# Steps of the conditioning products, moved from the heads of the latent-attention layer to the chunks of both attention output projections

## The chip, the cores and the metric

The kernel runs on one core of one Trainium2 chip. The metric is the device time of one execution in microseconds (us). The core has five engines with queues of their own: PE (TensorE) multiplies matrices, DVE (VectorE), ACT (ScalarE) and POOL (GpSimd) work elementwise on up to 128 rows, and SP (SyncE) here only issues transfers. PSUM holds the results of PE's products, SBUF everything else that is on the chip. L551 means line 551 of the kernel.

## The reference

A residual stream x of 512 tokens and 1024 features goes through three blocks. The first has causal attention with a forget gate ("fox"), the second has latent attention ("MLA"), and behind either stands a mixture of 16 experts with two of them for each token (MoE). A third block has a recurrence and a large table of experts. In each block six vectors that depend on the conditioning c scale, shift and gate what is done:

```python
    c_act = jax.nn.silu(c)
    for i in range(DEPTH):
        mod = c_act @ w_ada[i] + b_ada[i]
        sh1, sc1, g1, sh2, sc2, g2 = [m[:, None, :] for m in jnp.split(mod, 6, axis=-1)]
        h = rmsnorm(x, mix_norm[i]) * (1.0 + sc1) + sh1
        ...
        x = x + g1 * y
        h = rmsnorm(x, ffn_norm[i]) * (1.0 + sc2) + sh2
        x = x + g2 * hier_moe(h, moe_w_grp[i], moe_b_grp[i], moe_w_rt[i], moe_b_rt[i],
                              moe_w_gate[i], moe_w_up[i], moe_w_down[i])
```

The third block does the same with c_2, cond_w_2 and cond_b_2. Here y is the attention's output, o @ w_out. What is moved are products c_act @ w_ada and silu(c_2) @ cond_w_2: 48 columns of 128 features for each block.

## The kernel before

**Layout.** x stands in SBUF with the features on partitions, in 8 chunks of 128 features by 512 tokens. Products are taken in float32 as sums of three: each operand is split into a high part (`whi`, `o_hi`, on ACT) and what is left (`wlo`, `o_lo`, on DVE or POOL), and `mm3` multiplies high by high, low by high and high by low (L124 to L126).

**Conditioning.** `ada` (L157) is a generator that makes one column at a time: SP loads a tile `ada_w` of 128 by 1024 (512 KB), and DVE multiplies it by the silu row and sums along the row, L182; two steps later DVE adds the bias, L168. That is a step. There are three tiles `ada_w`, which lie in the pool that `self.ring` names, and loads run two steps ahead. 16 of the 144 columns are made when the kernel starts. The others, 128, are made one by one by `step(n)`, which the attention heads call (L392): 76 of them from the heads of the fox layer and 52 from those of the MLA layer. These 52 are the 4 x (2 + 2 + 2 + 7) of the tuple in the last line of `mla_heads`. The silu row of c_2, which the last 48 need, is thus made in the MLA heads; it and the row of c stand in the pool `cond`, which is closed before the MLA layer's output projection.

**Attention heads.** `heads` (L358) runs 16 heads in stages that are interleaved with their neighbours': PE makes the logits S, DVE takes the row's largest (`sm_mx`, L318), ACT exponentiates to P (L321), DVE divides (L325), PE transposes P (`tr`, L334), ACT copies (`pt`, L335), PE multiplies with the values (`pv`, L352), and ACT copies the head's result to `oT` (L353). Between the stages stands the preparation of the next four heads (a quarter).

**Output projection.** `out_proj` (L535 to L553) splits oT into `o_hi` and `o_lo`, eight tiles each, and makes 8 chunks of 24 products; DVE adds each chunk to x (L551). Behind a chunk, `then` makes ready what the MoE routes by: ACT squares x (`e_sq`, L838), DVE sums (`e_acc`, L840).

**MoE.** From x's last chunk a chain of small DVE operations runs to the lists of tokens: `n_v` and `n_r` (1 / rms), `lg` (logits), the two largest, `pos`, then PE's `pv` and DVE's `lst` (L945). Among them DVE also makes the normed rows (`n_t`, L263, and `h_row`, L961). The rows go to memory (`rows`, L964), and POOL gathers an expert's rows from there by its list (`hg`, L976). Ahead of the first gather each engine reads the count of the longest list and branches (L1104, L1105) past a part for lists that overflow. The first of the experts' weights are split ahead of that branch: seven splits `whi` on ACT, four of the `wlo` on POOL, three on DVE. POOL also numbers the tokens there (`tokens`, L1146).

**Order.** The order of each engine's instructions is set when the program is built, from what is ready first and from when a pool's memory comes free; an engine takes its queue in order.

## Time and profile before

| | us |
|---|---|
| median of 3 runs (lowest, highest) | 3077.49 (3072.53, 3083.78) |
| the profiled execution's span | 3077.5 |
| PE busy in it | 2764.6 |
| DVE busy | 2363.3 |
| ACT busy | 1314.5 |
| POOL busy | 1334.4 |

A row of the timeline gives the start, the duration, the engine, the line, the operation, what is written and what is read, and in square brackets how long the engine had been idle and what it had waited for. A row of a table by stretches gives busy times of the engines within it, the mean TensorE clock that was granted (1.00 is 2.4 GHz, 0.50 is 1.2 GHz), and the share of the DMA engines' time. The stretches of this case: the fox heads run to 368 us, their output projection to 420, the routing of the first MoE to 449. The MLA heads run from 715 to 934, their output projection to 988, the second routing to 1016.

### The profile page before, as it was taken

To read this page: it belongs to the slowest core of one execution; us is meant where nothing else is said; L and a number is where in the kernel's file an instruction comes from. 1 tells how busy PE (TensorE), PEld (TensorE's weight loads), DVE (VectorE), ACT (ScalarE), POOL (GpSimd) and SP (SyncE) were. 2 spreads that over 40 slices of the span, in tenths; PEclk is the share of its full clock that TensorE was granted. 3 is DMA by queue.
4 is the path that set the end of the run, shared out by engine and by line. 5 is a ranking of instruction groups with operands and counts; after the bars stand their busy time and mean duration, and the time that the engine had idled before them with its cause. 6 is when DMAs were issued, how large, how long until landed. Compare 5 with 4: busy or idle time off the path is not lost.

```text
span 3077.5 us, 42494 instructions
## 1 busy us (share of the span) xinstructions
PE 2764.6 (90%) x14989; PEld 2247.0 (73%) x14989; DVE 2363.3 (77%) x4756; ACT 1314.5 (43%) x2352; POOL 1334.4 (43%) x926
## 2 busy tenths in 40 slices
PE   2999978997889798899889897899999999999996
PEld 2877556686545566666766687889899999999885
DVE  7998458758975686688974799999677777777777
ACT  3344437734564573532432533334333333333332
POOL 3111027633211573006850345433566666666553
PEclk9999879998899899999988998999999999999998
DMA  6775159924535795220021223565999999999893
GB/s 220 239 242 182 65 193 314 342 96 139 185 124 188 236 331 205 90 72 19 1 78 37 88 85 122 201 227 185 322 312 321 313 318 325 326 314 315 285 328 112
DMA packets 230881, 622.81 MB, mean 202 GB/s; under 512 B 32796, under 2 KB 92492, under 8 KB 227192
## 3 DMA queue, kind: packets, MB, share of 16 engines
q1 hardware_dynamic: 130960, 429.82, 41.3%
q0 software_dynamic: 45120, 154.42, 14.7%
q10 hardware_dynamic: 54568, 35.66, 4.0%
q8 instruction: 122, 2.00, 0.3%
q14 instruction: 111, 0.91, 0.1%
HBM read 562.59 MB, written 61.01 MB: 203 GB/s over the span
## 4 chain that ended last, share of the span: by engine, by line
PE 39%; DVE 20%; DMA 4%; issue 2%; ACT 1%; POOL 1%; POOLq 0%; ACTq 0%; DVEq 0%; SPq 0%
PE y L126 5%; PE y L125 5%; PE acc L124 5%; PE acc L126 5%; PE acc L125 5%; PE y L124 5%; DVE a L1906 4%; DVE a L1902 2%; DMA wraw<-in_moe_w_dn_dram 2%; DMA wraw<-in_moe_w_gu_dram 2%; DVE s_y L1367 1%; DVE s_y L1526 1%; DVE wlo L118 1%; DVE wc L1550 1%; DVE t L1774 1%
## 5 line engine op out<-in xcount | busy, mean ns | idle before, releaser
L117 ACT ACTIVATE whi<-wraw 128x1024 fp32r<-128x1024 f32 (+1 forms) x552 | 576.5, 1049 | 458.2 <-PE acc L125 288.3
L118 DVE TENSOR_TENSOR wlo<-wraw,whi 128x1024 fp32r<-128x1024 f32 x410 | 565.5, 1390 | 265.6 <-ACT whi L117 264.4
L118 POOL TENSOR_TENSOR wlo<-wraw,whi 128x1024 fp32r<-128x1024 f32 (+1 forms) x142 | 367.1, 2592 | 478.9 <-ACT whi L117 445.2
L124 PE MATMUL acc<-h_hi,whi 128*128 128x384 f32 (+1 forms) x1328 | 478.0, 360 | 11.0 <-ACT z_out L1959 6.8
L126 PE MATMUL acc<-h_hi,wlo 128*128 128x384 f32 (+1 forms) x1328 | 472.5, 356 | 3.0 <-DVE wlo L118 3.0
L125 PE MATMUL acc<-h_lo,whi 128*128 128x384 f32 (+1 forms) x1328 | 473.1, 356 | 0.0
L126 PE MATMUL y<-whi,hid_l 128*128 128x512 f32 x768 | 302.3, 394 | 0.0
L1991 POOL DMA_INDIRECT gu<-in_peer_u_dram,e x128 | 206.5, 1613 | 219.0 <-DVE gu L2000 192.0
L125 PE MATMUL y<-wlo,hid_h 128*128 128x512 f32 x768 | 301.0, 392 | 0.0
L124 PE MATMUL y<-whi,hid_h 128*128 128x512 f32 x768 | 298.2, 388 | 0.0
L124 PEld LDWEIGHTS acc<-h_hi,whi 128*128 128x128 f32 x1328 | 255.1, 192 | 29.3 <-ACT z_out L1959 7.1
L126 PEld LDWEIGHTS acc<-h_hi,wlo 128*128 128x128 f32 x1328 | 254.4, 192 | 18.4 <-DVE wlo L118 4.0
L125 PEld LDWEIGHTS acc<-h_lo,whi 128*128 128x128 f32 x1328 | 255.1, 192 | 16.7 <-issue 1.0
L1991 POOL DMA_INDIRECT gv<-in_peer_v_dram,e x128 | 191.7, 1497 | 37.6 <-issue 27.6
L2056 ACT ACTIVATE hid_h<-hid 128x384 fp32r<-128x384 f32 x128 | 67.1, 524 | 289.2 <-PE y L125 252.7
L2032 DVE SCALAR_TENSOR_TENSOR y<-gv,pz,y 128x1024 f32<-128x1024 f32 x128 | 181.2, 1416 | 0.0
L182 DVE SCALAR_TENSOR_TENSOR ada_w<-ada_w,silu 128x1024 f32<-128x1024 f32 x138 | 174.0, 1261 | 8.7 <-DMA ada_w<-in_w_ada_dram 8.6
L125 PEld LDWEIGHTS y<-wlo,hid_h 128*128 128x128 f32 x768 | 144.2, 188 | 30.3 <-DVE wlo L118 0.3
L126 PEld LDWEIGHTS y<-whi,hid_l 128*128 128x128 f32 x768 | 144.3, 188 | 29.1
L124 PEld LDWEIGHTS y<-whi,hid_h 128*128 128x128 f32 x768 | 144.2, 188 | 28.8
L124 PE MATMUL acc<-whi,h_hi 128*128 128x256 f32 x480 | 140.6, 293 | 26.9 <-ACT whi L117 18.7
L2000 DVE SCALAR_TENSOR_TENSOR gu<-gu,hrow 128x1024 f32<-128x1024 f32 x128 | 163.2, 1275 | 0.0
(671 smaller groups left out, 6246.6 us busy)
## 6 DMA issues: line engine op xcount, KB each, us to landing
ada_w<-in_w_ada_dram SPq DMA_DIRECT2D x144, 512.0 KB, 4.2
wraw<-in_moe_w_gu_dram SPq DMA_DIRECT2D x128, 512.0 KB, 10.9
wraw<-in_peer_ut_dram SPq DMA_DIRECT2D x128, 512.0 KB, 6.3
wraw<-in_peer_v_dram SPq DMA_DIRECT2D x128, 512.0 KB, 5.9
wraw<-in_moe_w_dn_dram SPq DMA_DIRECT2D x64, 512.0 KB, 12.3
p_gd<-stage SPq DMA_DIRECT2D x24, 1024.0 KB, 3.9
gt<-p_gd ACTq DMA_DIRECT2D x16, 1536.0 KB, 22.0
wraw<-in_fox_w_in_dram SPq DMA_DIRECT2D x24, 512.0 KB, 4.7
```

The costliest lines, as they stand in the source:

```text
L117: nc.scalar.activation(hi[:, :w], r[:, :w], AF.Copy)
L118: self.low = eng.tensor_tensor(lo[:, :w], r[:, :w], hi[:, :w].bitcast(F32), op=OP.subtract).ins
L124: mm(out=out, lhsT=l[0], rhs=r[0], start=start, stop=False)
L125: mm(out=out, lhsT=l[0], rhs=r[1], start=False, stop=False)
L126: mm(out=out, lhsT=l[1], rhs=r[0], start=False, stop=stop)
L182: V.scalar_tensor_tensor(r, r, 1.0, c, op0=OP.mult, op1=OP.mult, accum_out=m)
L1902: V.tensor_tensor(a1, io[:, None, :].to_broadcast([128, 8, 128]), tr[:, 0, t0:t0 + 8, None].to_broadcast([128, 8, 128]), op=OP.is_equal)
L1906: V.tensor_scalar(a2[:, t, :], io, tr[:, 1, t0 + t:t0 + t + 1], tr[:, 2, t0 + t:t0 + t + 1], op0=OP.is_equal, op1=OP.mult)
L1991: nc.gpsimd.indirect_dma_start(out=u, out_offset=None, in_=src[:, :], in_offset=bass.IndirectOffsetOnAxis(ap=e3[:, k:k + 1], axis=0))
L2000: V.scalar_tensor_tensor(u, u, 1.0, hrow, op0=OP.mult, op1=OP.mult, accum_out=z8[b][:, k % 8:k % 8 + 1])
L2032: V.scalar_tensor_tensor(y3, vs.pop(k), z8[k // 8][:, k % 8:k % 8 + 1], y3, op0=OP.mult, op1=OP.add)
L2056: nc.scalar.activation(hh, hid, AF.Copy)
```

## The change

The MLA heads are given 4 x (0 + 0 + 1 + 4) = 20 steps in place of 52. Each output projection makes two steps behind each of its 8 chunks, 16 in all; for that it names its own pool as the one that holds `ada_w`. On the last step ahead of a pool's end the loads run only one step ahead. The pool `cond` stands on the other side of SBUF, and is closed behind the MLA layer's output projection. The rest of the diff takes away comments, so that lines move down by 1 to 7 numbers.

```diff
-            while len(rs) < min(k + bufs - 1, len(cols)):
+            while len(rs) < min(k + (bufs - 1 if self.prefetch else 1), len(cols)):
...
-    def step(self, n):
-        for _ in range(n):
+    def step(self, n, last=False):
+        for k in range(n):
+            self.prefetch = not last or k < n - 1
             next(self.aside)
...
-                self.step((k + 1) * n // 4 - k * n // 4 if k < 4 else 0)
+                self.step((k + 1) * n // 4 - k * n // 4 if k < 4 else 0, last and k == 3)
...
-    def out_proj(self, x, oT, w, g1, pool, then=None):
+    def out_proj(self, x, oT, w, g1, pool, then=None, steps=0):
+        self.ring = pool
         o = self.split(oT, pool, "o")
...
             nc.vector.scalar_tensor_tensor(x[:, c, :], ps, g1[:, c:c + 1], x[:, c, :], op0=OP.mult, op1=OP.add)
+            self.step(steps, c == 7)
+        self.ring = None
...
-        self.heads(quart, oT, pool, (2, 2, 2, 7), 2, rest)
+        self.heads(quart, oT, pool, (0, 0, 1, 4), 2, rest)
...
-                self.out_proj(x, oT, self.A["fox_w_out"], mod[:, 16:24], p, then=then())
+                self.out_proj(x, oT, self.A["fox_w_out"], mod[:, 16:24], p, then=then(), steps=2)
...
-            self.cond.close()
             with self.pool("m_out") as p:
-                self.out_proj(x, oT, self.A["mla_w_out"], mod[:, 16:24], p, then=then())
+                self.out_proj(x, oT, self.A["mla_w_out"], mod[:, 16:24], p, then=then(), steps=2)
+        self.cond.close()
...
-        cond = self.cond.enter_context(self.pool("cond", "right"))
+        cond = self.cond.enter_context(self.pool("cond"))
```

Three places show how the built program's queues moved. The first is DVE in the MLA heads, about the eighth head, where a quarter's queries are prepared (`rq`, `qk_ss`). Before:

```order
L168 TENSOR_TENSOR mod_116<-bias,ada_t 128x1
L182 SCALAR_TENSOR_TENSOR ada_w,ada_t<-ada_w,silu 128x1024
L323 RECIPROCAL sm_r<-sm_s 128x1
L168 TENSOR_TENSOR mod_116<-bias,ada_t 128x1
L182 SCALAR_TENSOR_TENSOR ada_w,ada_t<-ada_w,silu 128x1024
L740 TENSOR_TENSOR rq<-acc,mla_gq 128x384 x2
L325 TENSOR_SCALAR P<-P,sm_r 128x512
L168 TENSOR_TENSOR mod_116<-bias,ada_t 128x1
L182 SCALAR_TENSOR_TENSOR ada_w,ada_t<-ada_w,silu 128x1024
L168 TENSOR_TENSOR mod_116<-bias,ada_t 128x1
L182 SCALAR_TENSOR_TENSOR ada_w,ada_t<-ada_w,silu 128x1024
```

And now:

```order
L326 RECIPROCAL sm_r<-sm_s 128x1
L321 TENSOR_REDUCE sm_mx<-S 128x1
L326 RECIPROCAL sm_r<-sm_s 128x1
L328 TENSOR_SCALAR P<-P,sm_r 128x256
L321 TENSOR_REDUCE sm_mx<-S 128x1
L326 RECIPROCAL sm_r<-sm_s 128x1
L328 TENSOR_SCALAR P<-P,sm_r 128x384
L747 TENSOR_TENSOR rq<-acc,mla_gq 128x384 x2
L321 TENSOR_REDUCE sm_mx<-S 128x1
L326 RECIPROCAL sm_r<-sm_s 128x1
L328 TENSOR_SCALAR P<-P,sm_r 128x512
```

No step is left there: DVE's queue holds the 20 that remain ahead of the fifth head's last `sm_mx`, where 18 of the 52 stood before.

The second is PE at the end of the fox layer's heads, where the last head's `tr` and `pv` meet the first chunk of the output projection (`acc`). Before:

```order
L124 MATMUL acc<-o_hi,whi 128x512 x2
L334 MATMUL tr<-ident,P 128x128 x3
L125 MATMUL acc<-o_lo,whi 128x512
L126 MATMUL acc<-o_hi,wlo 128x512
L124 MATMUL acc<-o_hi,whi 128x512
L334 MATMUL tr<-ident,P 128x128 x4
L125 MATMUL acc<-o_lo,whi 128x512
L126 MATMUL acc<-o_hi,wlo 128x512
L124 MATMUL acc<-o_hi,whi 128x512
L125 MATMUL acc<-o_lo,whi 128x512 x2
L352 MATMUL pv<-pt,v 64x512
```

And now:

```order
L337 MATMUL tr<-ident,P 128x128 x7
L858 MATMUL tr<-wr_117,mod_114 128x20 x8
L355 MATMUL pv<-pt,v 64x512
L355 MATMUL pv<-pt,v 64x384
L355 MATMUL pv<-pt,v 64x256
L355 MATMUL pv<-pt,v 64x128
L125 MATMUL acc<-o_hi,whi 128x512 x2
L126 MATMUL acc<-o_lo,whi 128x512
```

The whole first chunk now stands behind the last head's `pv`, because `o_hi` and `o_lo` lie in memory that the heads' `pt` takes up (the pool `cond` pushed them there); ACT's and DVE's splits of oT moved with it. At the end of the MLA heads it stood so before already.

The third is POOL between the fox heads (`qk_two`) and the branch of the first MoE. Before:

```order
L118 TENSOR_TENSOR wlo<-wraw,whi 128x1024 x4
L1084 MEMSET y_zero 128x1024
L932 IOTA io_4480 128x104
L1146 IOTA tokens 128x512
L1104 TENSOR_LOAD cnt_i
```

And now:

```order
L1091 MEMSET y_zero 128x1024
L939 IOTA io_4561 128x104
L1153 IOTA tokens 128x512
L119 TENSOR_TENSOR wlo<-wraw,whi 128x1024 x4
L1111 TENSOR_LOAD cnt_i
```

The four splits moved from the output projection to behind `tokens`, into the routing. ACT's seven `whi` moved with them, two of them right behind the logits' `lt` and at least three behind the issue of the rows, and DVE's three `wlo` stand right ahead of the branch now. The reason is SP's queue, where the loads of these weights stand behind those of the 16 steps, in memory that the projection's tiles leave. At the second MoE the moves are the same.

## Rows read from the trace of the kernel before

**Rows 1.** Stretch, length; PE, PEld, DVE, ACT, POOL busy; PEclk; DMA; GB/s.

```profile
814.73:898.57 83.84, 70.66 (x315) 43.20 (x316) 73.71 (x207) 46.61 (x127) 15.37 (x10) 0.88 0.52 165
898.57:924.04 25.47, 23.44 (x114) 12.92 (x115) 10.78 (x33) 17.06 (x48) 0.00 (x0) 1.00 0.22 74
```

**Rows 2.** The same stretch, DVE's L182 alone.

```profile
814.73:898.57 83.84, 31.84 (x52) 0.88 0.52 165
```

**Rows 3.** What PE waited for from 814.73 to 898.57: us, times, longest.

```profile
PE tr L334 <- DVE P L325: 10.4, 4, 3.6
```

**Rows 4.** Timeline, PE and DVE, from the last fox head to the projection.

```profile
363.47 0.60 PE L334 MATMUL tr<-ident,P 128*128 128x128 f32 x4
...
371.56 0.75 DVE L551 SCALAR_TENSOR_TENSOR x<-acc,mod,x 128x512 f32<-128x512 f32 x1 [1.96 <-PE acc L126]
...
377.55 0.62 PE L851 MATMUL tr<-wr,mod 128*128 128x20 f32 x4
```

**Rows 5.** Timeline, PE and DVE, the same place of the MLA layer.

```profile
926.94 0.63 PE L334 MATMUL tr<-ident,P 128*128 128x128 f32 x4 [1.55 <-DVE P L325]
...
929.20 4.06 PE L352 MATMUL pv<-pt,v 128*64 128x512 f32 x8
...
941.05 0.75 DVE L551 SCALAR_TENSOR_TENSOR x<-acc,mod,x 128x512 f32<-128x512 f32 x1 [1.51 <-PE acc L126]
```

**Rows 6.** Timeline, DVE, one chunk of the fox output projection and the next's start.

```profile
398.74 0.75 DVE L551 SCALAR_TENSOR_TENSOR x<-acc,mod,x 128x512 f32<-128x512 f32 x1 [3.07 <-PE acc L126]
...
400.54 0.69 DVE L840 TENSOR_TENSOR e_acc<-e_acc,e_sq 128x512 f32<-128x512 f32 x1 [1.05 <-ACT e_sq L838]
401.49 1.23 DVE L118 TENSOR_TENSOR wlo<-wraw,whi 128x1024 fp32r<-128x1024 f32 x1 [0.26 <-ACT whi L117]
405.50 0.75 DVE L551 SCALAR_TENSOR_TENSOR x<-acc,mod,x 128x512 f32<-128x512 f32 x1 [2.79 <-PE acc L126]
```

**Rows 7.** Timeline, POOL and DVE side by side, in that projection and in the MLA heads.

```profile
402.48 11.00 POOL L118 TENSOR_TENSOR wlo<-wraw,whi 128x1024 fp32r<-128x1024 f32 x4 [66.29 <-ACT whi L117]
407.96 6.60 DVE L118 TENSOR_TENSOR wlo<-wraw,whi 128x1024 fp32r<-128x1024 f32 x2
...
729.54 0.73 POOL L596 TENSOR_TENSOR rp<-rq,sin 128x256 f32<-128x256 f32 x1
729.65 0.65 DVE L142 TENSOR_TENSOR qk_r_z<-qk_r_y 128x16 f32<-128x16 f32 x1
```

**Rows 8.** Timeline, all engines, the first MoE's routing.

```profile
419.02 0.75 DVE L551 SCALAR_TENSOR_TENSOR x<-acc,mod,x 128x512 f32<-128x512 f32 x1 [2.06 <-PE acc L126]
...
435.07 0.47 DVE L263 SCALAR_TENSOR_TENSOR n_t<-x,n_a,acc 128x256 f32<-128x256 f32 x1
...
435.62 0.66 DVE L961 COPY h_row<-S 128x512 f32<-128x512 f32 x1
...
436.36 3.03 ACTq L964 DMA_DIRECT2D rows<-h_row  x4
...
443.89 0.16 DVE L945 CAST lst<-pv 104x16 int32<-104x16 f32 x1
...
448.68 1.08 POOL L976 DMA_INDIRECT hg<-rows,lst  x1 [26.03 <-issue]
...
455.19 1.28 ACT L986 ACT_TABLE_LOAD   x1 [18.56 <-PE tr L984]
...
461.18 2.39 POOL L118 TENSOR_TENSOR wlo<-wraw,whi 128x1024 fp32r<-128x1024 f32 x1 [4.09 <-ACT whi L117]
```

**Rows 9.** Timeline, DVE and POOL, the second MoE's list and first gather.

```profile
1011.78 0.17 DVE L945 CAST lst<-pv 104x16 int32<-104x16 f32 x1
1016.09 1.11 POOL L976 DMA_INDIRECT hg<-rows,lst  x1 [25.50 <-DVEq L1105]
```

**Rows 10.** Part 6 of the page: loads of a step, KB each, us to landing.

```profile
ada_w<-in_w_ada_dram SPq DMA_DIRECT2D x144, 512.0 KB, 4.2
```

**Rows 11.** As in the first group, in the first MoE.

```profile
540.00:560.00 20.00, 19.31 (x95) 13.86 (x94) 16.37 (x19) 16.63 (x23) 14.91 (x9) 1.00 1.03 343
```

More of the change, by code (lines that the diff above doesn't have):

```diff
@@ L30, in __init__ @@
         self.ring, self.more, self.over, self.extra, self.turn, self.ahead = None, None, None, {}, {}, {}
+        self.prefetch = True
         self.holds, self.hold = [], None
```

## The prediction

> **What bounds the kernel now.** I read the busy shares first: PE is busy for 2764.6 of 3077.5 us, DVE for 2363.3, so neither is the bound everywhere, and what the change is worth must be read where it acts. Then I cut the MLA heads into stretches [rows 1]. In the later one, where no step is made, three heads take 25.47 us, 8.49 each, with PE at 23.44 of 25.47 and at full clock: PE sets the pace. From 814.73 to 898.57 seven heads take 83.84 us, and DVE is busy for 73.71 of them, PE for 70.66 at a mean granted clock of 0.88. The longest waits of PE there are for P, which DVE divides late [rows 3], since it has 26 steps in its queue (52 instructions of L182, two for each) [rows 2]. Both lose: PE waits, and what it does afterwards runs at the lower of its two clocks. Then I read the places the steps go to. In a projection's chunk, 6.76 us from one x to the next, DVE is busy for 0.75 + 0.69 + 1.23 = 2.67 us [rows 6], so there is room for two steps. Last I read what comes behind, the routing, in which a single chain decides when the first gather starts, and the MoE behind it, which has no slack to catch up: in its middle DMA is busy throughout (1.03) and PE for 19.31 of 20 us [rows 11]. So a later first gather is paid in full.
>
> **The MLA heads: -13 us (-18 to -4).** Before the fifth head ends, 20 steps stand where 18 stood, so I give the stretch to 814.73 nothing. From there to 898.57, 26 steps go: 31.84 us of L182, 1.22 each [rows 2], and an addition of about 0.17 each (the size of `lst` in [rows 8]), 4.4 us. DVE falls from 73.71 to some 37 of 84 us. Then PE is the bound. Its 70.66 us at clock 0.88 are 62.2 at full clock; with the 8% that it idles in the stretch without steps (2.03 of 25.47, [rows 1]) that is 67.6 us, 16.2 less than now. That is nearly the best case; the quarters' preparation stays, with its long way over DVE and POOL, and some of the low clock with it. The lower bound is that only the wait on P is cut, by less than half of its 10.4 us [rows 3]: -4. I take -13, nearer to the stretch without steps, because DVE will be as idle as it is there for half the heads.
>
> **The end of the fox heads: +4 (0 to +6).** Now the first chunk's products fill PE while the last head's P is made; from the last `tr` to the first x it takes 371.56 - 363.47 = 8.1 us [rows 4]. After the change all 24 products stand behind `pv`, which is the form that the MLA layer has now, and there the same takes 941.05 - 926.94 = 14.1 [rows 5], with `pv` itself at the lower clock (4.06 us). The difference is 6.0, less about 2.0 for four repeats of `tr<-wr,mod`, which leave the projection's middle: one such row of four takes 0.62 [rows 4], and there are sixteen. The MLA layer's end has that form before and after: nothing.
>
> **Steps in the projections: +3 (0 to +7).** Two steps cost DVE 2 x (1.22 + 0.17) = 2.8 us a chunk; with 2.67 that is 5.5 of 6.76. It fits on the mean, and PE hides it, as long as each `wlo` comes before PE needs it. In the new order some `wlo` stand behind two steps; I allow one stall of about the 1.4 us of a step in either projection. A step's 512 KB land in 4.2 us [rows 10], and two of them have a chunk of 6.76 us: nothing. In the fox projection ACT also makes silu of c_2, with a table load of 1.28 us more [rows 8]; ACT's own work on a chunk is a square and a split, each about as long as DVE's part of it, so that it has the room: nothing.
>
> **The two routings: +5 and +6 (-2 to +12 each).** This is what speaks most against the change. Seven splits leave the projections and stand in the routing. The profile shows what that does to DVE: while POOL ran four splits back to back, two `wlo` on DVE took 6.60 us instead of 2 x 1.23, and while POOL ran operations of 0.73 us, one of DVE's smallest took 0.65 [rows 7] instead of the 0.16 of `lst` [rows 8]: it waits until POOL's instruction is done. What has an operand in PSUM, as x, keeps its 0.75: that at 405.50 stands in the middle of POOL's four [rows 6]. The chain `n_v`, `n_r`, `lg` is of such small operations in SBUF, and POOL's first two splits of 2.39 us [rows 8] fall on it: +4.8. The third falls on the later chain, and I count it in full: +2.4. On the other side a `wlo` of 1.23 no longer stands ahead of `n_v`, and in the first routing four copies `h_row` of 0.66 and two `n_t` of 0.47 [rows 8] move behind `pos`: -1.2 and -3.6. One more table load on ACT, ahead of `ge`, costs 1.3 [rows 8]. The first list, at 443.89 now, comes 4.8 + 2.4 - 1.2 - 3.6 + 1.3 = 3.7 later. But the rows can be sent only behind the copies that moved: the last goes some 3 us behind the list, where it now goes ahead of it (436.36, [rows 8]), and a transfer of that size takes some 4.2 us to land [rows 10]; from list to gather there are 4.8 us [rows 8]. So the gather is bound by the list or by the rows, between +3.7 and 3.7 + 3 + 4.2 - 4.8 = +6.1: +5. In the second routing the copies stay ahead of the list: 4.8 + 2.4 - 1.2 = +6 on 1011.78 and on the gather at 1016.09 [rows 9]. The ends: if POOL's splits fall where DVE waits anyway, as at `pv`, the routing gets shorter by up to 2; if ACT also waits for the weights behind `lt`, +12.
>
> A rule bears on this. The Trainium skill, "SBUF — State Buffer", section "Who interferes with whom", says that DVE and GpSimd share one pair of SBUF ports, which is locked for a whole instruction, and that a DVE operation with two inputs in SBUF then waits, while a reduction or one with a single SBUF input does not. The 6.60 us in [rows 7] agree with it. By that rule the reductions and the `n_t` of the later chain would pass, the third split would cost nothing there, and the sum would be 2 x 2.4 less: 3078 in place of 3082.
>
> **Sum.** -13 + 4 + 3 + 5 + 6 = +5 us on a span of 3077.5, which is also the median of the runs (3077.49): 3082.5.
>
> **Rivals.** (1) *Faster, 3066.* POOL's splits find gaps. What speaks for it: DVE waits for PE and ACT in the routing too, the `n_t` with an operand in PSUM pass, and copies leave the first chain. Then the routings cost nothing, -16 + 4 + 1 + 0 = -11. Against it: the chain has hardly a gap ahead of `lg`, just where two splits become ready. It decides by when the first `wlo` on POOL starts: it is true if that is before `n_v` or behind `lg`. (2) *Slower, 3093.* The weights come late. They are loaded behind the last steps' tiles now, by my estimate from about 413 us, and the branch needs all seven splits; ACT's last three stand behind the rows. If ACT's two `whi` behind `lt` (some 2.5 us behind x's last chunk at 419.02, [rows 8]) wait for their load, `ge` and every `h_f` stand behind them, and the gather comes 10 to 12 us later in either routing: -13 + 4 + 3 + 11 + 11 = +16. It decides at a landing of 421.5. For it: 16 steps' loads and the last weights share the queue; against it: there are 8 us, and a load lands in 4.2 [rows 10]. (3) *The steps were not what held the heads, 3091.* PE then still waits for the preparation's way over POOL, the heads give 4, and the sum is -4 + 4 + 3 + 11 = +14. For it: the clock falls where a quarter is prepared. (4) *The change does not do what it says*, so that the same steps stay in the heads: the built order excludes that, no step stands behind the fifth head.
>
> **How the numbers follow.** 0.3%, 9.2 us, is about what a measurement of this kernel can tell from no change. My sum lies inside it with 4 us to its upper bound, so that much of its own spread is slower. I give the sum as it stands 0.46, rival 1 0.22, rival 2 0.20, rival 3 0.12. All of rival 1 is faster, rivals 2 and 3 and 0.02 of the sum's own spread are slower: faster 0.22, same 0.44, slower 0.34. The range reaches to rival 1 and rival 2 and a little beyond: 3064 to 3096.
>
> **What would show it.** After the change: seven heads from the fifth on in about 70 us, at a clock near 1.00; x at 6.8 us a chunk in both projections; from the last fox `tr` to the first x 12 to 14 us; POOL's splits between 422 and 441 us with `n_r` and `lg` stretched beside them; from x's last chunk to the first gather 34 to 36 us in the first layer instead of 448.68 - 419.02 = 29.7 [rows 8], and as much more in the second. I am wrong if the gather is not later (then POOL's splits do not meet the chain), or if the seven heads still take over 78 us (then something else than steps holds P).

## The result: slower, and where the time went

The changed kernel takes 3102.63 us (median of 4 runs, 3090.01 to 3116.11) against 3080.64 of the kernel before (4 runs, 3072.53 to 3089.66): a ratio of 1.0065, with an interval from 1.0036 to 1.0095. It is slower by about 20 us. The forecast was 3082.5, and the time lies above the range's end of 3096. Its profiled execution has a span of 3088.3 us, 10.8 more than that of before.

The page of the changed kernel opens with the busy time, share of the span and instructions of each engine:

```profile
PE 2756.0 (89%) x14989; PEld 2240.0 (73%) x14989; DVE 2365.4 (77%) x4756; ACT 1316.5 (43%) x2354; POOL 1319.6 (43%) x926
```

PE is busy for 8.6 us less than before, DVE for 2.1 and ACT for 2.0 us more, so no engine has much more work; what grew is waiting. To find it I cut both traces at the same events and compare the lengths. The table gives the core's times in us; the events are the starts of `x`, the residual of a projection's chunk, of `hg`, the first gather of an MoE, and of `oT`, the end of a head.

| stretch | before | after | difference | forecast |
|---|---|---|---|---|
| start to the last fox `oT` | 367.6 | 370.4 | +2.8 | 0 |
| to the first `x` | 3.9 | 8.4 | +4.5 | +4 |
| to the eighth `x` | 47.5 | 45.2 | -2.3 | +1.5 |
| to the first gather | 29.7 | 37.5 | +7.8 | +5 |
| first MoE, to the latent rows | 239.0 | 244.9 | +5.9 | 0 |
| MLA: to the end of the first head | 68.5 | 76.7 | +8.2 | |
| MLA: four more heads | 58.5 | 51.1 | -7.4 | 0 with the line above |
| MLA: the seven heads behind | 83.8 | 70.3 | -13.5 | -13 |
| MLA: the last four | 34.7 | 33.5 | -1.2 | 0 |
| to the first `x` | 7.8 | 8.4 | +0.6 | 0 |
| to the eighth `x` | 45.9 | 45.2 | -0.7 | +1.5 |
| to the second gather | 29.1 | 34.2 | +5.1 | +6 |
| second MoE, to the third block | 233.4 | 236.3 | +2.9 | 0 |
| the rest | 1828.0 | 1826.1 | -1.9 | 0 |

The first line varies by itself, and another profile of the kernel before has 363.8 there; but its last head belongs to the change, as is shown below. The two MoEs' lines are the ones for which the forecast has no price.

**The heads.** The windows of the changed kernel below have the columns of [rows 1]; they run to the end of the first head, over four more, and over the seven behind them. The second fence is the last of them with L183 alone, the line that was L182 in [rows 2]:

```profile
706.43:783.10 76.67, 58.66 (x320) 46.55 (x318) 65.25 (x174) 31.35 (x82) 27.53 (x20) 0.93 0.41 129
783.10:834.23 51.13, 44.77 (x214) 29.86 (x213) 44.97 (x134) 30.24 (x82) 14.61 (x10) 0.93 0.39 123
834.23:904.52 70.29, 63.81 (x314) 38.91 (x315) 39.13 (x121) 45.84 (x126) 11.26 (x10) 1.00 0.03 8
```

```profile
834.23:904.52 70.29, 0.00 (x0) 1.00 0.03 8
```

The seven heads have no step, DVE is busy for 39.13 us instead of 73.71, the granted clock is 1.00 instead of 0.88, and they take 70.29 us instead of 83.84 [rows 1]. PE's wait for the P that DVE divides, at the head of its list before [rows 3], is gone. The head of the list is now a wait for ACT, which frees S when it has made P from it, and it is short (us, times, longest):

```profile
PE S L795 <- ACT P L324: 3.6, 4, 1.2
PE tr L337 <- ACT st L790: 1.6, 5, 0.4
```

**The end of the fox heads.** PE's timeline and the first `x`, as in [rows 4]:

```profile
362.49 0.69 PE L337 MATMUL tr<-ident,P 128*128 128x128 f32 x4 [0.48 <-DVE P L328]
362.97 3.44 PE L858 MATMUL tr<-wr,mod 128*128 128x20 f32 x16
366.35 4.04 PE L355 MATMUL pv<-pt,v 128*64 128x512 f32 x8
371.72 0.73 PE L125 MATMUL acc<-o_hi,whi 128*128 128x512 f32 x2 [1.33 <-ACT o_hi L538]
378.81 0.74 DVE L556 SCALAR_TENSOR_TENSOR x<-acc,mod,x 128x512 f32<-128x512 f32 x1
```

It now has the form of the MLA layer's end [rows 5]: the router's transposes, `pv` of 4.04 us, 1.33 us in which PE waits for the split of oT, and then all 24 products. The table's 4.5 us, from the last head's `oT` on, are not all of it, since that `oT` is late itself. These are the last two heads' `oT`, first before and then in the changed kernel:

```profile
358.94 0.59 ACT L353 ACTIVATE oT<-pv 64x512 f32<-64x512 f32 x1 [4.48 <-PE pv L352]
367.62 0.59 ACT L353 ACTIVATE oT<-pv 64x512 f32<-64x512 f32 x1 [1.30 <-PE pv L352]
```

```profile
358.44 0.59 ACT L356 ACTIVATE oT<-pv 64x512 f32<-64x512 f32 x1 [1.83 <-PE pv L355]
370.42 0.59 ACT L356 ACTIVATE oT<-pv 64x512 f32<-64x512 f32 x1 [6.55 <-PE pv L355]
```

Up to the head before the last the changed kernel is 0.5 us ahead; the last head then takes 11.98 us instead of 8.68. From the last but one `oT` to the first `x` it is 20.37 instead of 12.62, so the end of the heads costs 7.8 us, 3.3 of which stand in the table's first line. All three profiles of the changed kernel have 11.98 or 11.99 for the last head, both of the kernel before 8.5 to 8.7.

**The first routing.** POOL, DVE and ACT, as in [rows 8]:

```profile
424.02 0.75 DVE L556 SCALAR_TENSOR_TENSOR x<-acc,mod,x 128x512 f32<-128x512 f32 x1 [4.55 <-PE acc L127]
426.39 1.99 ACT L118 ACTIVATE whi<-wraw 128x1024 fp32r<-128x1024 f32 x2
427.37 0.16 DVE L255 TENSOR_SCALAR n_v<-misc 128x4 f32<-128x4 f32 x1 [1.15 <-PE misc L214]
428.37 4.66 POOL L119 TENSOR_TENSOR wlo<-wraw,whi 128x1024 fp32r<-128x1024 f32 x2
428.37 0.16 DVE L145 SCALAR_TENSOR_TENSOR n_r_y<-n_r_z,n_r_y 128x4 f32<-128x4 f32 x1
428.56 2.19 DVE L143 TENSOR_TENSOR n_r_z<-n_r_y 128x4 f32<-128x4 f32 x1
430.79 2.26 DVE L144 SCALAR_TENSOR_TENSOR n_r_z<-n_r_z,n_v 128x4 f32<-128x4 f32 x1
433.28 0.16 DVE L143 TENSOR_TENSOR n_r_z<-n_r_y 128x4 f32<-128x4 f32 x1
433.94 0.24 DVE L871 TENSOR_TENSOR lg<-S,n_r_y 128x80 f32<-128x80 f32 x1
448.42 5.40 ACTq L971 DMA_DIRECT2D rows<-h_row  x4
450.54 0.16 DVE L952 CAST lst<-pv 104x16 int32<-104x16 f32 x1
454.96 3.50 DVE L119 TENSOR_TENSOR wlo<-wraw,whi 128x1024 fp32r<-128x1024 f32 x3 [1.47 <-ACT whi L118]
461.55 1.08 POOL L983 DMA_INDIRECT hg<-rows,lst  x1 [11.31 <-issue]
471.43 1.62 PE L991 MATMUL tr<-ident,hg 104*128 104x104 f32 x8 [18.73 <-DMA hg<-rows,lst]
```

Beside POOL's two splits two operations of 128x4 elements take 2.19 and 2.26 us; the first of them takes 0.16 when it comes again at 433.28. The list comes 26.52 us behind `x`, against 443.89 - 419.02 = 24.87 [rows 8], so that part is only 1.65 late. From list to gather it is 11.01 us against 4.79 [rows 8]. What POOL waits for last ahead of the gather is DVE, until 460.55: DVE's branch stands behind its three splits (454.96 to 458.46), these behind ACT's `whi`, and those behind the issue of the rows. The last rows have landed by 458.53. And then comes what I had no term for: the gathered rows reach PE's `tr` 471.43 - 461.55 = 9.9 us after the gather is issued. Before it was 5.5, as this row with 448.68 of [rows 8] says:

```profile
454.19 1.62 PE L984 MATMUL tr<-ident,hg 104*128 104x104 f32 x8 [10.43 <-DMA hg<-rows,lst]
```

What runs beside it is in the DMA share and the GB/s of the windows (last two columns): first the kernel before around its gather, then the changed kernel around both of its own.

```profile
448.00:455.00 7.00, 0.81 (x5) 0.84 (x6) 0.81 (x2) 0.00 (x0) 2.08 (x2) 0.50 0.41 123
```

```profile
455.00:472.00 17.00, 0.57 (x4) 0.61 (x5) 4.34 (x5) 1.82 (x2) 2.07 (x2) 0.50 0.79 264
1025.00:1037.00 12.00, 0.70 (x4) 0.73 (x5) 0.72 (x2) 0.00 (x0) 2.02 (x2) 0.50 0.94 298
```

The gather used to run nearly alone; now it shares the DMA engines with the loads of the MoE's next weights. In the second window of after 68.7% of the engines' span goes to the queue of the loads and 24.3% to that of the gathers. PE has no other work meanwhile: 0.70 us of 12. All thirteen profiles of this document agree on it. In 12 of their 26 routings packets of the loads run between the gather's issue and PE's `tr`, and take 70 to 77% of the engines' time there: the landing takes 9.5 to 11.2 us. In the other 14 that queue has no packet there: 5.0 to 6.3 us.

**Why the loads are there.** The section on the change says that `o_hi` and `o_lo` lie in memory of the heads' `pt`. That was wrong; the addresses in the built program say what is right. A step in a projection needs its tiles `ada_w` in the projection's own pool, three of them. Two end at byte 152544 of a partition. The third reaches to 156640, over the start of the fox heads' pool (153568) and over the first tile of the MoE's weights (from 153120). By the third tile alone the pool's first loads are placed behind the fox heads, with the split of oT behind the last head's `pv`, and in both layers the weights' loads are placed behind the last step. (In the MLA layer `o_lo` lies over the heads' pool, before and after.) So 3.5 KB of a partition, shared by one tile of the steps and one of the weights, push the whole queue of weights back. The kernel with two tiles, below, shows that it is this tile.

### The profile page after: what moved, and what is told of

Same layout as the page of the kernel before. It is cut to its first block, busy times and chain, and to the rows that moved or that the text cites. A ratio compares the mean times of both kernels' runs of the same rounds, so it can differ in the third digit from the quotient of the medians.

```text
span 3088.3 us, 42493 instructions
## 1 busy us (share of the span) xinstructions
PE 2756.0 (89%) x14989; PEld 2240.0 (73%) x14989; DVE 2365.4 (77%) x4756; ACT 1316.5 (43%) x2354; POOL 1319.6 (43%) x926
## 4 chain that ended last, share of the span: by engine, by line
PE 39%; DVE 19%; issue 2%; DMA 2%; POOL 2%; ACT 1%; POOLq 0%; ACTq 0%; DVEq 0%
PE y L127 5%; PE y L126 5%; PE acc L126 5%; PE acc L127 5%; PE y L125 5%; PE acc L125 5%; DVE a L1913 4%; DVE a L1909 2%; DVE s_y L1374 1%; DMA wraw<-in_moe_w_dn_dram 1%; DVE s_y L1533 1%; DVE wlo L119 1%; POOL wlo L119 1%; DVE wc L1557 1%; DVE t L1781 1%
## 5 line engine op out<-in xcount | busy, mean ns | idle before, releaser
L119 DVE TENSOR_TENSOR wlo<-wraw,whi 128x1024 fp32r<-128x1024 f32 x410 | 558.9, 1374 | 257.6 <-ACT whi L118 254.6
L125 PE MATMUL acc<-h_hi,whi 128*128 128x384 f32 (+1 forms) x1328 | 476.8, 359 | 10.8 <-ACT z_out L1966 6.5
L126 PEld LDWEIGHTS acc<-h_lo,whi 128*128 128x128 f32 x1328 | 254.2, 191 | 16.3 <-issue 0.8
L1998 POOL DMA_INDIRECT gv<-in_peer_v_dram,e x128 | 191.0, 1492 | 37.6 <-issue 27.3
L183 DVE SCALAR_TENSOR_TENSOR ada_w<-ada_w,silu 128x1024 f32<-128x1024 f32 x138 | 173.6, 1259 | 15.6 <-DMA ada_w<-in_w_ada_dram 12.9
L127 PEld LDWEIGHTS y<-whi,hid_l 128*128 128x128 f32 x768 | 144.3, 188 | 29.1
```

Source lines behind the costliest of these rows:

```text
L119: self.low = eng.tensor_tensor(lo[:, :w], r[:, :w], hi[:, :w].bitcast(F32), op=OP.subtract).ins
L125: mm(out=out, lhsT=l[0], rhs=r[0], start=start, stop=False)
L126: mm(out=out, lhsT=l[0], rhs=r[1], start=False, stop=False)
L127: mm(out=out, lhsT=l[1], rhs=r[0], start=False, stop=stop)
L183: V.scalar_tensor_tensor(r, r, 1.0, c, op0=OP.mult, op1=OP.mult, accum_out=m)
L1998: nc.gpsimd.indirect_dma_start(out=u, out_offset=None, in_=src[:, :], in_offset=bass.IndirectOffsetOnAxis(ap=e3[:, k:k + 1], axis=0))
```

## The experiments

My theory behind the result, A in the expectations, was that the steps themselves hide in the projections, that the heads keep their gain, and that the loss comes from the third tile: the end of the fox heads, the late splits and the late loads. The rivals there blame the steps, wherever they stand, or the splits on POOL. Each ratio below is against the kernel before on the same chip. The table has the stretches of the one above, for the profiled execution of each kernel: the MLA heads in one sum, with the first in brackets, and behind each gather its landing, from the issue to PE's `tr`.

| kernel | fox `oT` to `x` | eight `x` | gather | its landing | first MoE | MLA heads (first) | eight `x` | gather | its landing | span | ratio |
|---|---|---|---|---|---|---|---|---|---|---|---|
| before | 3.9 | 47.5 | 29.7 | 5.5 | 239.0 | 245.5 (68.5) | 45.9 | 29.1 | 5.2 | 3077.5 | |
| after | 8.4 | 45.2 | 37.5 | 9.9 | 244.9 | 231.6 (76.7) | 45.2 | 34.2 | 10.5 | 3088.3 | 1.0065 |
| mla_only | 3.9 | 47.5 | 29.9 | 5.5 | 238.6 | 244.2 (67.4) | 45.2 | 34.2 | 10.2 | 3079.4 | 1.0054 |
| fox_only | 9.0 | 45.9 | 37.7 | 9.9 | 247.9 | 243.3 (76.8) | 45.9 | 29.7 | 5.5 | 3111.3 | 1.0086 |
| two_tiles | 3.9 | 54.5 | 37.4 | 5.2 | 240.3 | 236.7 (77.4) | 50.5 | 31.7 | 5.2 | 3092.8 | 1.0042 |
| light_heads | 3.9 | 47.5 | 30.1 | 5.0 | 239.6 | 232.2 (65.1) | 45.9 | 29.8 | 6.3 | 3067.7 | 0.9976 |
| dve_splits | 8.4 | 45.2 | 31.9 | 9.6 | 243.4 | 235.9 (76.1) | 45.9 | 31.9 | 10.1 | 3091.5 | 1.0064 |
| held | 8.4 | 45.2 | 37.5 | 9.5 | 245.6 | 227.3 (60.7) | 45.2 | 34.3 | 10.0 | 3088.8 | 1.0044 |
| two_held_dve | 3.9 | 48.6 | 34.5 | 5.4 | 241.1 | 226.3 (63.1) | 46.7 | 30.9 | 5.1 | 3070.6 | 0.9977 |
| held52 | 3.9 | 47.5 | 29.9 | 5.5 | 242.2 | 243.9 (63.6) | 45.9 | 29.8 | 5.5 | 3092.9 | 1.0003 |

**The same kernel again**, beside the next three.

> The changed kernel once more, to see what lies between its profiled execution (span 3088.3 us, 10.8 over before) and the median of its runs (22 over). If the difference between its executions is noise of the MoE's or the third block's transfers, a second profile has the same times up to the second routing (last fox oT to x(7) 53.6 us, x(7) to the first gather 37.5 us, gather to the latent rows 245 us) and differs behind it. If one of the moved pieces varies, one of those three differs by several us. The ratio to before should be 1.003 to 1.008.

Measured: 3101.29 us against 3084.35, 1.0074 [1.0053, 1.0095], 6 runs. The loss stands. Its profile (span 3096.6) has the same stretches from the first `x` to the second gather within 1 us; it is 3.8 us longer in the second MoE and 3.1 in the third block. Its gathers land in 10.5 and 11.2 us.

**Only two tiles in the projections**, so that the pool reaches over neither the heads' pool nor the weights. The loads then run one step ahead instead of two.

```diff
-            while len(rs) < min(k + (bufs - 1 if self.prefetch else 1), len(cols)):
-                r = self.ring.tile([128, D], F32, tag="ada", bufs=bufs, name="ada_w")
+            n = self.tiles or bufs
+            while len(rs) < min(k + (n - 1 if self.prefetch else 1), len(cols)):
+                r = self.ring.tile([128, D], F32, tag="ada", bufs=n, name="ada_w")
...
-        self.ring = pool
+        self.ring, self.tiles = pool, 2
```

> As the change, but the projections' pool has two tiles ada_w instead of three, so that it ends 568 bytes short of where the heads' pool and the MoE's weights begin, and laps over neither. Theory A (the third tile's overlap did the harm: it pushed the first chunk, the weights' loads and the splits back): from the last fox oT to x(7) 51 to 53 us, x(7) to the first gather 29 to 31 us in both layers, gather to the latent rows 239 us, the heads keep their gain of 14: 3062 to 3068 us by the profile, ratio 0.994 to 0.998. Theory B (the steps' own 2.8 us of DVE and 1 MB of loads for each chunk did it): no better than the change, 3088 or more, ratio 1.003 or more.

Measured: 3093.77, 1.0042 [1.0017, 1.0067]. What A says of the tile came true: the end of the fox heads is back at 3.9 us (the last head at 8.5), and the gather's landing at 5.2. But the gain did not come, because the weights then arrive early again and POOL's splits meet the steps. POOL and DVE in the fox projection:

```profile
404.67 9.15 POOL L119 TENSOR_TENSOR wlo<-wraw,whi 128x1024 fp32r<-128x1024 f32 x3 [62.90 <-DMA ada_w<-in_w_ada_dram]
404.82 3.43 DVE L184 SCALAR_TENSOR_TENSOR ada_w<-ada_w,silu 128x1024 f32<-128x1024 f32 x1
408.18 3.39 DVE L184 SCALAR_TENSOR_TENSOR ada_w<-ada_w,silu 128x1024 f32<-128x1024 f32 x1
413.83 0.74 DVE L557 SCALAR_TENSOR_TENSOR x<-acc,mod,x 128x512 f32<-128x512 f32 x1
...
465.93 1.08 POOL L984 DMA_INDIRECT hg<-rows,lst  x1 [32.74 <-SPq L1113]
```

A step's product takes 3.43 us there instead of 1.22, two in a row hold `x` back, and the eight `x` take 54.5 us instead of 47.5. The first gather stays late as well, at 37.4 us, though its list is on time, 24.9 us behind `x` as before: now the loads of the weights run beside the rows that the gather reads. The last rows are issued at 454.96 and landed at 464.80, when POOL's wait for them ends, and the last three take 8.7 to 10.6 us; in the changed kernel the last took 5.0, with no load beside it. So A in that form fell: the third tile is one part of the loss, and without it the early weights cost elsewhere, POOL's splits beside the steps and the loads beside the rows. With three tiles these two are absent, since the weights come too late to meet them.

**Steps in one projection only**, with 36 left in the heads.

```diff
-        self.heads(quart, oT, pool, (0, 0, 1, 4), 2, rest)
+        self.heads(quart, oT, pool, (1, 1, 2, 5), 2, rest)
```

together with `steps=2` taken from the fox projection (mla_only) or from the MLA projection (fox_only).

> 16 steps go to the MLA layer's projection alone, and 36 stay in its heads, 4 x (1 + 1 + 2 + 5). The third tile laps over the second MoE's weights alone. Theory A: fox layer, first routing and first MoE as before; heads gain about half, 5 to 8; second routing 5 later: 3073 to 3079 us. Theory B: the loss is that of one projection's steps: about half of the change's 11 to 20, with the heads' half gain in it: 3080 to 3088.

> 16 steps go to the fox layer's projection alone, and 36 stay in the MLA heads. Theory A: x(7) 5 later, first gather 8 more, first MoE 6 more, heads gain 5 to 8, second routing as before: 3088 to 3092 us, as slow as the whole change or slower. Theory B: half of the change's loss, 3080 to 3088.

Measured: mla_only 3095.07, 1.0054 [1.0033, 1.0074]; fox_only 3111.45, 1.0086 [1.0054, 1.0118]. The profiles put each cost where its steps stand: mla_only has the late gather (34.2) and the slow landing (10.2) in the second layer alone, fox_only has 9.0, 37.7 and 9.9 in the first, and in the second 29.7 and 5.5 as before. The heads gain 1 to 2 us with 36 steps, not the 5 to 8 that A expects, and less than the 4.1 by which two profiles of the kernel before differ there. So both times are above A's (3073 to 3079, and 3088 to 3092). fox_only also shows something that belongs to the heads: its first MLA head ends late (76.8), that of mla_only does not (67.4). mla_only's profiled execution is the fastest of its six, and its ratio is worse than its profile's 2 us by an amount that no stretch of that profile explains. Of the 33.8 us that fox_only's span is longer, 9.8 stand in the third block, which no edit touches.

**Fewer steps, none of them in the projections.** Its expectation says what is left out.

```diff
-                self.out_proj(x, oT, self.A["mla_w_out"], mod[:, 16:24], p, then=then(), steps=2)
+                self.out_proj(x, oT, self.A["mla_w_out"], mod[:, 16:24], p, then=then())
```

and the same in the fox projection.

> The heads of the change, 4 x (0 + 0 + 1 + 4) steps, and none in the projections: 32 columns of the third block's conditioning are left out and stand at zero. It measures what the heads alone gain. The row of c_2 is again made among the heads, so that by the built order 6 steps stand ahead of the first head and not 8. Theory C (the change's first head came 8 us later, 76.7 instead of 68.5 from the latent rows, because silu of c_2 was ready and more steps slipped into the first quarter's preparation): latent rows to first head 67 to 69, to the last head 222 to 228 instead of 245.6, all else as before, 3055 to 3062 us. Theory D (the first head is late for another reason, such as the pools' places): again 76 to 78, 231 to the last head, 3062 to 3067.

Measured: 3073.06 against 3078.91, 0.9976 [0.9958, 0.9994]. With the projections, routings and MoEs as before, 20 steps in the heads are worth 13.3 us of their span (245.5 to 232.2), which is the term of the forecast, measured alone. Against the second profile of the kernel before, with 241.5, it is 9.3, and the medians of the runs differ by 5.9. The span, 3067.7, is above the 3055 to 3062 that I expected. The first head is at 65.1: here its silu is made in the heads again.

**The first expert's splits on DVE instead of POOL**, in both layers.

```diff
-            w = self.weight(A["moe_w_gu"][l, e, k], eng=nc.gpsimd if k == 3 or (first and k < 3) else None, key=(e, k))
+            w = self.weight(A["moe_w_gu"][l, e, k], eng=nc.gpsimd if k == 3 and not first else None, key=(e, k))
```

> As the change, with the first expert's splits on DVE instead of POOL, so that POOL runs no split in the routing. If POOL's splits hold up the chain (my prediction's step): n_v to lg takes 2.4 us instead of 6.6, and the list stands 22 to 23 us behind x(7) instead of 26.5 in the first layer; the gather 33 to 35 us behind x(7) instead of 37.5, unless the rows or the branch, ahead of which DVE now has seven splits, bind it. If the chain is held by something else, n_v to lg stays 6 to 7 us. Total 3083 to 3089 by the profile.

Measured: 3093.21, 1.0064 [1.0035, 1.0093]. DVE, POOL and PE in the first routing:

```profile
427.19 0.16 DVE L255 TENSOR_SCALAR n_v<-misc 128x4 f32<-128x4 f32 x1 [1.15 <-PE misc L214]
429.63 0.24 DVE L871 TENSOR_TENSOR lg<-S,n_r_y 128x80 f32<-128x80 f32 x1
455.78 1.08 POOL L983 DMA_INDIRECT hg<-rows,lst  x1 [27.56 <-issue]
465.38 1.62 PE L991 MATMUL tr<-ident,hg 104*128 104x104 f32 x8 [15.76 <-DMA hg<-rows,lst]
```

From `n_v` to `lg` it is 2.4 us again instead of 6.6, so POOL's splits are shown to stretch that part of the chain. The gather comes 31.9 us behind `x` instead of 37.5, but in the first layer the list is only 0.6 us earlier, since DVE now makes three splits of 1.22 us ahead of it. The other 5.0 us lie between list and gather, where the rows go out 6 us earlier and DVE reaches its branch earlier. In the second layer the list is 3.2 us earlier and the gather 2.3. So moving the splits brings the gathers forward, and only the second layer's gain is the chain's. The landing stays at 9.6 us, since the loads still run beside it. In the profiled execution the 5.6 and 2.3 us that the routings gave are used up by the last heads (+4.1, and the third profile of the changed kernel has the same 37.6 there) and the second MoE (243.1 us), and the ratio is that of the changed kernel. The span is above the 3083 to 3089 that I expected. So the gain in place is shown, a gain in time is not.

**No step ahead of the first score**: the steps of the MLA heads are held in the order behind the `sm_mx` of the head they were placed at.

```diff
-            nc.vector.tensor_reduce(mx, s[:, :n], axis=AX.X, op=OP.max, negate=True)
+            self.mark = nc.vector.tensor_reduce(mx, s[:, :n], axis=AX.X, op=OP.max, negate=True).ins
...
-                self.step((k + 1) * n // 4 - k * n // 4 if k < 4 else 0, last and k == 3)
+                with self.tc.issue_after(self.mark) if steps[0] == 0 else contextlib.nullcontext():
+                    self.step((k + 1) * n // 4 - k * n // 4 if k < 4 else 0, last and k == 3)
```

> As the change, but each step of the MLA heads is queued on DVE behind its own head's largest value: none stands ahead of the first head, one each in heads 9 to 12, four each in the last four. Theory C: latent rows to first head 60 to 68 us instead of 76.7, to the last head 220 to 228 instead of 231.6; all else as in the change; 3078 to 3084 us by the profile. Theory D: first head at 76 as in the change, and the last four heads slower by the steps: 3088 to 3092.

Measured: 3090.07, 1.0044 [1.0022, 1.0067]. The stretch to the end of the first head, L183 alone, in the changed kernel and then here:

```profile
706.43:783.10 76.67, 12.17 (x19) 0.93 0.41 129
```

```profile
710.10:770.70 60.60, 0.00 (x0) 0.97 0.27 84
```

It shrinks from 76.7 to 60.7 us. The changed kernel has 19 records of L183 there (two for each step), the kernel before 14 of L182. The fox projection makes silu of c_2 ahead of the MLA layer, so nothing holds these steps any more, and more of them are placed ahead of the first head's scores, on DVE's way to the queries. Of the 16 us the four heads behind give back 6.2, and the last four 5.2, so that the time is above the 3078 to 3084 that I expected.

**All three together**: two tiles, held steps, splits on DVE.

> Two tiles in the projections (no overlap), steps held to their heads, and the first expert's splits on DVE, so that POOL's do not meet the steps' products in the projections. If the three causes are the third tile, the steps in the preparation, and POOL's splits against DVE's steps: fox oT to x(7) 51 to 54 us (58.4 with two tiles and POOL's splits), x(7) to the gather 30 to 33, latent rows to the last head 220 to 228, last head to x(7) 54 to 56; 3058 to 3068 us, ratio 0.993 to 0.998. If it is the steps' load on DVE and DMA in any form, the projections stay at 56 or more and the total over 3075.

Measured: 3072.71 against 3078.91, 0.9977 [0.9958, 0.9995], 12 runs. The interval just excludes 1, so it is faster than the kernel before, and by way of that than the changed kernel (1.0065 and 1.0074). The first gather and its landing in it:

```profile
456.35 1.08 POOL L985 DMA_INDIRECT hg<-rows,lst  x1 [30.89 <-SPq L1114]
461.79 1.62 PE L993 MATMUL tr<-ident,hg 104*128 104x104 f32 x8 [16.17 <-DMA hg<-rows,lst]
```

The heads give 19.2 us; the routings still cost 4.8 and 1.8, and the projections 1.1 and 0.8. In the first routing POOL's last wait is for the rows: the last of them is issued at 446.42 and landed at 455.31, 8.9 us later, again with loads of weights beside it. Its time is above the 3058 to 3068 that I expected.

**All 52 steps in the heads, but held**: heads (3, 3, 3, 4), none in the projections.

> No step in the projections; all 52 stay in the MLA heads, 4 x (3 + 3 + 3 + 4), each queued on DVE behind its own head's largest value, and the pool cond on the side the change gave it. If what matters is where the steps stand and not how many there are: the projections, routings and MoEs as in the kernel before, latent rows to first head 60 to 65 instead of 68.5, and the sixteen heads 168 to 177 us (177.1 before): 3066 to 3076 us. If the heads need fewer steps: 3076 to 3086, with the heads at 178 or more.

Measured: 3085.79 against 3084.54, 1.0003 [0.9981, 1.0025]. The heads take 243.9 us, 1.6 less than before, and from the first head's end to the last's 180.3 us, above the 168 to 177 that I expected. The first head gains (63.6), the fifth to eleventh still have their steps. The first five heads together take 127.3 us (127.0 before), the seven behind them gain 7.3, and the last four lose 5.4. So moving the 52 steps within the heads moves the time among them and hardly changes the sum.

**Both kernels once more**, one run each on that chip.

> The kernel before once more, for a second profile: how far do its stretches repeat? From the second gather to the third block's first product 233 to 234 us if that stretch is steady and the 236 to 240 of the change are its own; 233 to 240 if it only varies from run to run. Latent rows to first head 68 to 69, first gather to latent rows 239 to 240.

> The changed kernel for a third profile. If both MoE stretches are longer in it by their own (the weights come late): first gather to latent rows 244 to 246, second gather to the third block 236 to 241. If they only vary: values down to 239 and 233 as in the kernel before.

Measured: 3080.06 and 3091.82. The stretches to the second gather repeat within 4.2 us in each; behind it the same kernel differs from run to run (the second MoE of the kernel before takes 233.4 and 236.2 us).

**What stays open.** Three profiles of the changed kernel have a mean span of 3091.7, two of the kernel before 3077.9: 13.8 us. The timed difference is 22 us on one chip and 17 on another. The stretches above account for the 10.8 us of the first pair, and two_held_dve, which takes the third tile, the steps ahead of the first score and POOL's splits away together, is below the kernel before in time as well. Where the rest of the timed difference lies, no profile shows: behind the second gather the stretches vary from run to run, and the third block took 1828.1 and 1832.0 us before and 1826.1, 1829.2 and 1822.3 after. I have no run that ties that rest to a cause.

## Why the prediction was wrong, step by step

**Heads, -13: right.** 245.5 to 231.6 is -13.9, the seven heads in 70.3 us at a clock of 1.00. The seven repeat (82.4 in the second profile before, 70.3 in all three after), the sixteen less well: the means of all profiles, 243.5 and 233.2, differ by some 10. The step "to the fifth head: nothing" came out at +0.8 as a sum, +8.2 and -7.4, but for a reason that it does not give, and held shows that it hides a possible gain.

**End of the fox heads, +4: too small,** and wrong in the cause that the section on the change names. From the last `tr` to the first `x` it is 378.81 - 362.49 = 16.3 us where 12 to 14 were forecast, and from the last but one `oT` on it is +7.8. The forecast took the transposes `tr<-wr,mod` off as leaving the projection's middle. They do leave it, but now stand ahead of `pv`, where they take 3.44 us; and two steps of 1.22 us stand on DVE ahead of the first `x`. two_tiles, with `o_hi` where it was and only the third tile gone, has the last head and the 3.9 us of before.

**Projections, +3: too much.** They got shorter by 3.0, since the transposes left the fox layer's and the splits left both, and the steps hid, as the chunk of 6.8 us said they would. From the last but one `oT` to the eighth `x` the fox layer is 5.5 longer, which is the forecast of both terms, 4 + 1.5, by luck: the end is dearer than forecast and the projection cheaper. The bound of a stall behind two steps is real, but only where POOL splits at the same time (two_tiles, +7.0).

**Routings, +5 and +6: +7.8 and +5.1.** In the second the pieces can be read one by one: `n_v` 0.6 earlier, `n_v` to `lg` 4.2 longer (forecast 4.8), from `lg` to the list 0.7 longer (forecast 2.4 for the third split), and 0.75 more from list to gather. Beside that third split one small operation, `e_e`, takes 1.18 us instead of 0.17, while the `n_t` beside it, with an operand in PSUM, keep 0.47. The rule that I weighed, the Trainium skill, "SBUF — State Buffer", section "Who interferes with whom", says that only an operation that needs DVE's second port waits; the trace agrees, and by it the third split's price would have been nearer. In the first routing the list was only 1.65 late, and the last rows are issued 3.3 us behind it (forecast 3) and landed 5.0 later (forecast 4.2, [rows 10]). But neither list nor rows set the gather, as the prediction says: POOL's last wait is for DVE, until 460.55, 2.0 us behind the rows' landing. The prediction has no term for the three splits that DVE makes ahead of the branch, which stand behind the rows by way of ACT's queue.

**The MoEs, 0: the step that failed.** The prediction says that a later first gather is paid in full, and its sum has no term for anything else that changes behind it. The first half holds, the second does not: the gather itself lands in 9.9 and 10.5 us instead of 5.5 and 5.2, because the loads that the third tile pushed behind the branch run beside it. The first MoE is 5.9 us longer, the second 2.9, with the landing's 4.4 and 5.3 in them. mla_only and fox_only show this in the layer that has steps and in that alone, two_tiles in none. The lengths agree over all profiles: with the slow landing the first MoE takes 243.4 to 247.9 us and the second 236.3 to 243.1, without it 238.6 to 242.2 and 232.4 to 236.2. The prediction knew that the weights are loaded late (rival 2) and looked for the cost in ACT's `whi` ahead of the list; those ran without a wait, at 426.39. The mechanism was priced in the wrong place.

**The sum.** Heads and routings came out with the sign and about the size that were forecast. The end of the fox heads and the projections did not, and their errors cancel: -13.9 + 7.8 - 3.0 + 7.8 + 5.1 = +3.8 in the profile instead of +5, close by luck. The missing term adds 8.8, the rest of the table -1.8, and the profile is 10.8 longer. None of the rivals came true by its own sign: POOL's first split, at 428.37, falls between `n_v` and `lg` (1), ACT's `whi` did not wait (2), and the heads gave 14 (3). The missing term alone would have put the forecast at 3091, inside its range, and the profiled execution is inside it too (3090.01). It is the fastest of its four, and their median is 12.6 higher: by that spread the time left the range, and what makes it stays open.

## What to carry to other kernels

Work that is moved takes its buffers along: look where they lie, since a few KB that reach over another pool can reorder a whole queue of loads and everything that hangs on it. Price what is pushed aside to the end, past the wait that you are looking at: a load that comes late costs again as the neighbour of the next transfer that the bound engine waits for. And a gain that is right in its place (14 us in the heads) has to be held against each place that the work goes to; here, of the forms that were tried, the same move pays only with two tiles, the splits off POOL and the steps behind the first score together, and then by 0.2%.

## What the runs showed of the hardware

A gather of 104 rows took 5.0 to 6.3 us from issue to PE's first use where no backlog of loads ran (14 routings; 123 GB/s around it in the kernel before), and 9.5 to 11.2 us beside one (12 routings; 264 to 298 GB/s in the changed kernel). Rows that were sent to memory beside such loads landed 8.7 to 10.6 us after their issue in two_tiles; the last rows of the changed kernel, with no such load beside them, landed after 5.0. An operation of 4 elements in a partition can take 2.26 us on DVE instead of 0.16 beside a split on POOL, and a step's product of 128x1024 took 3.43 instead of 1.22; operations that read PSUM kept their times beside it (`n_t` 0.47, `x` 0.75 in [rows 6]). A `pv` of eight products behind short transposes ran 4.04 us at a granted clock of 0.58, as in the MLA layer before [rows 5]; before the change the fox layer's took 2.37 at 1.00.
